# Router logits from the raw residual sums, and two weight pieces split ahead in borrowed places

## The chip, the cores and the metric

The program runs on one core of one Trainium2 chip. Its engines work side by side, each through its own instruction stream in order: TensorE (PE, with its weight loads PEld), VectorE (DVE), ScalarE (ACT), GpSimd (POOL) and SyncE (SP), which starts the weight transfers. The metric is the device time of one execution in microseconds (us), as a median over runs; lower is better.

## What is computed

Two layers over 256 rows of 1024 columns: layer 0 is a mixer and a dense SwiGLU; layer 1 is a gated DeltaNet mixer and a mixture of 8 SwiGLU experts, of which every row uses the best two. After each of the four sublayers comes `x <- LayerNorm(alpha * x + f(x))`. What the change touches is the end of the DeltaNet and the head of the experts:

```python
h = mixer_gated_deltanet(x, ...)                     # ends in  o @ w_out
x = layer_norm(ALPHA * x + h, c_ln1_g, c_ln1_b)      # (r - mean) * rstd * g + b
logits = x @ w_router + b_router                     # (256, 8)
top_val, top_idx = lax.top_k(logits, 2)
gates = softmax(top_val)
y = sum over e of combine[:, e] * swiglu(x, w_gu[e], w_down[e])
x = layer_norm(ALPHA * x + y, c_ln2_g, c_ln2_b)
```

With the raw sum `r = ALPHA * x + h`, its row mean and `rstd`, the logits are also `rstd * (r @ (g * w_router)) - mean * rstd * colsum(g * w_router) + colsum(b * w_router) + b_router`.

## The kernel before

The 256 rows are two blocks of 128 (block 0 and 1). Every float32 product runs as three matmuls: weights and activations are split into a rounded high part and the rest (`wh`, `wl`; `xh`, `xl`), ACT writing the high part and DVE (in a few places POOL) the low part. Weights come in pieces of 1 MB (`wraw`), started by SP in program order into raw places, 15 of them by the time of the experts; each piece is split in two halves of 1024 columns, which PE uses one after the other. The split halves live in a ring of five pairs of places, two of them in a pool that ends with the dense part, so three for the experts. The emitted order is made when the kernel is built: `presplit` splits ahead as far as the ring allows, and small pieces of work (the chunks of the DeltaNet, gathers, expert activations) are generators that `tick` puts between weight matmuls when a simple estimate of engine times (`Pace`) says that their inputs are ready. So a small piece that is added to the DeltaNet shifts where many later ones are put.

The DeltaNet starts with projections and a small chain (`sm`: decays and betas) and ends with `out_proj`: for each of the eight row groups k of the output weights PE multiplies block 0; block 1 follows at once for k below 4, and the last four k of block 1 come in `late`. `sublayer_end` then takes each block through `ln_block`: residual sum and statistics on DVE, square root on ACT, then the normalising steps shared by DVE, ACT and POOL. The normalised block is transposed by PE (`transposed`, four 128x128 transposes for each half) and copied to `xt` by ACT.

`route` takes it from there: eight router matmuls a block (`logits`, 8 columns each), the comparison of all pairs of logits on DVE (`chosen`: `e3`, `cnt`, `sel`), a count of the rows chosen ahead (`count` on PE), `slot` and the one-hot matrices `S` (`places`, `onehot` on DVE). Fills (`self.fill`, matmuls of the identity with itself whose result nobody reads) stand in between on PE. `natural_parts` makes the high and low parts `xnh` (ACT) and `xnl` (POOL) of the normalised block. PE then gathers the rows of experts 0 and 1 with `S` (`gather_block`, quarters 0 to 3, each with `xnh` and `xnl`), ACT and DVE copy them to `xgh` and `xgl`, and the first expert's gate and up matmuls begin as soon as two quarters are there (`G0 = 2`). One more half of weights is split ahead in the places `hh` and `hl` by `extra`, POOL writing its low part. `gates` computes the weights of the two experts: maximum and difference on DVE, exponential on ACT, then the switch of ACT to the table of the expert activation.

Of the kernel before, what the change touches and what calls it, by code (L numbers as in the profile page):

```python
# [16 lines left out]
T = 256  # L17
# [4 lines left out]
NE = 8  # L22
# [87 lines left out]
LQ = 4  # L110
HV = 512
SP0 = 640
SP3 = 1024
MG = -300.0
GT = 3
FI = 6, 3, 3
# [116 lines left out]
class Columns:  # L233

    def __init__(self, tiles):
        self.tiles = tiles

    def __getitem__(self, k):
        return self.tiles[k[2].start // 512]


class Net:
# [288 lines left out]
    def sublayer_end(self, pt, n, table, between=None, early=1, plain=False, split=None):  # L531
# [7 lines left out]
        if plain:  # L539
            xh, lo = lambda b, q: self.xpart(self.xt, b, q), lambda b, q: None  # L540
        else:
            lo = lambda b, q: nc.vector.tensor_sub(xl(b, q), tv[b, q], xh(b, q))
# [22 lines left out]
        if between:  # L565
            between(r, ready)
        else:
            for q in range(2):
                ready(1, q)
        self.x = r  # L570
# [43 lines left out]
    def out_proj(self, key, oh, ol, wait):  # L614
# [14 lines left out]
        for k in range(KT):  # L629
# [403 lines left out]
    def load_g1(self):  # L1033
# [12 lines left out]
        self.g1 = cwn, nea, dtb  # L1046

# [127 lines left out]
    def mixer1(self):  # L1175
# [44 lines left out]
        def prologue():  # L1220
# [3 lines left out]
            nc.vector.tensor_copy(cw, t[:, 0:96])  # L1224
            self.give()
# [383 lines left out]
        pt = self.out_proj("wo1", oh, ol, wait)  # L1609
        self.ring = [r for r in self.ring if r[0] is self.spl]  # L1610
        self.NSPL -= self.NDENSE
        self.xt = self.keep.tile([P, KT, T], F32, name="xt", tag="xh")
        self.e3 = self.keep.tile([P, 2048], F32, name="e3", tag="xl")[:, 0:2 * NE * NE].rearrange("p (b e f) -> p b e f", b=2, e=NE)
        self.sublayer_end(pt, 3, "natural_log_exp_and_others", self.route, plain=True, split=(SP0, SP3))
# [26 lines left out]
    def moe_open(self):  # L1641

        nc, a, tc = self.nc, self.a, self.tc
        self.raw_pool("raw2", RO)
        self.load_next()
        self.mo = mo = self.ctx.enter_context(tc.tile_pool(name="mo", bufs=1))
        self.wr = mo.tile([P, KT, NE], F32, name="wr")
        nc.gpsimd.dma_start(self.wr, a["moe_w_router"].rearrange("(k p) e -> p k e", p=P))
        self.br = mo.tile([P, NE], F32, name="br")
        nc.gpsimd.dma_start(self.br, a["moe_b_router"].partition_broadcast(P))  # L1650
# [17 lines left out]
    def route(self, r, ready):  # L1668
# [3 lines left out]
        tt, mm, X = nc.vector.tensor_tensor, nc.tensor.matmul, mybir.AxisListType.X  # L1672
        lg, e3, sel = self.lg, self.e3, self.sel
        p = self.ps("A")
        s = self.first = self.new_s()

        def logits(b, ks=range(KT)):
            for k in ks:
                mm(p[:, b * NE:(b + 1) * NE], self.xt[:, k, b * P:(b + 1) * P], self.wr[:, k], start=k == b == 0,
                   stop=k == KT - 1, skip_group_check=True)  # L1680

        def chosen(b):
            tt(lg[:, b], p[:, b * NE:(b + 1) * NE], self.br, OP.add)
            yield
            tt(e3[:, b], lg[:, b][:, None, :].to_broadcast([P, NE, NE]), lg[:, b][:, :, None].to_broadcast([P, NE, NE]),
               OP.subtract)
            yield
            tt(e3[:, b], e3[:, b], c("tie").rearrange("p (e f) -> p e f", e=NE), OP.is_gt)
            yield
            nc.vector.tensor_reduce(self.cnt[:, b], e3[:, b], axis=X, op=OP.add)  # L1690
            yield
            nc.vector.tensor_scalar(sel[:, b], self.cnt[:, b], 1.5, None, OP.is_lt)

        def count(b, m, start, stop):
            mm(p[:, (2 + b) * NE:(3 + b) * NE], m, sel[:, b if m is self.tri else 0], start=start, stop=stop,
               skip_group_check=True)

        def places(b):
            nc.vector.scalar_tensor_tensor(self.slot[:, b], p[:, (2 + b) * NE:(3 + b) * NE], 1.0, sel[:, b], OP.add, OP.mult)
            yield  # L1700
            for j in range(2):
                self.onehot(s, j, lambda b: self.slot[:, b, j:j + 1], (b,))
                yield

        fill = lambda n: self.fill(c("ident"), n)
        fill(FI[0])
        logits(0)
        self.natural_parts(0, r[0])
        ready(1, 0)
        fill(FI[1])  # L1710
        ready(1, 1)
        for _ in chosen(0):
            pass
        logits(1, range(0, LQ))
        count(0, self.tri, False, True)
        count(1, self.one, False, False)
        logits(1, range(LQ, KT))
        fill(FI[2])
        self.natural_parts(1, r[1])
        steps = [chosen(1), places(0)]  # L1720
        while steps:
            for g in list(steps):
                if next(g, 1):
                    steps.remove(g)
        self.early = [self.ps("B") for _ in range(4)]
        self.live += 4
        for i, t in enumerate(self.early):
            if i == 2:
                count(1, self.tri, False, True)
            self.gather_block(t, (self.xnh, self.xnl)[i % 2], s, i // 2, 0)  # L1730
        for _ in places(1):
            pass
        self.presplit(1)
        for b in range(2):
            nc.scalar.activation(r[b], r[b], AF.Copy, scale=ALPHA)
# [39 lines left out]
    def gather(self, s, xg, got, early=()):  # L1775

# [3 lines left out]
        early = list(early)  # L1780
        yield from self.when(s, slack=MG)
        for q in range(4):
            for i, xn in enumerate((self.xnh, self.xnl)):
                if early:
                    p = early.pop(0)
                else:
                    p = yield from self.take()
                    self.gather_block(p, xn, s, q, 0)
# [157 lines left out]
    def extra(self):  # L1946

        tiles = []
        for _ in range(2):
            for t in self.new_parts():  # L1950
                pass
            tiles.append(self.parts)
        self.ring.insert(0, (None, tiles))
        self.held = -1
        self.presplit(1, self.nc.gpsimd)

    def extra_done(self):
        self.hfree += 2

    def moe(self):  # L1960
# [15 lines left out]
        def prep(e):  # L1976
            xs = [self.new_xg() for _ in range(2)]
            xg[e], xg[e + 1] = xs
            yield from self.gather(S[e], xs, got[e], self.early if e == 0 else ())
# [9 lines left out]
        next(first)  # L1989
        self.extra()  # L1990
# [8 lines left out]
        self.y = self.x  # L1999

        def mult(e, c, u, after):
            pt = [self.ps("A") for _ in range(c[1] // 512)]
            n = 8 if c[1] == 1024 else 4
            for j in range(n):
                w = self.next(("gu", e, c, u))
                then = (lambda: after(pt)) if j == n - 1 else None
                if isinstance(w[0], Columns):
                    self.held, then = 0, self.extra_done
# [191 lines left out]
```

## Time and profile before

| | us |
|---|---|
| median of 3 runs | 1598.83 (1598.19 to 1599.57) |
| the profiled execution | 1597.8 |
| its span | 1596.0 |
| TensorE busy, sum of the page | 1555.4 |
| VectorE / ScalarE / GpSimd busy | 1301.3 / 1050.6 / 160.5 |

All rows are of the one profiled execution; times are counted from the start of its span. A timeline row gives the start, the duration, the engine, the operation with what it writes and reads, how many instructions it joins, and in brackets the idle time just before it with what ended that. On PE one logical float32 matmul is two instructions. A row of windows gives for one stretch its length, then busy time (and instructions) of PE, PEld, DVE, ACT and POOL, the granted TensorE clock as a share of 2.4 GHz, the busy share of the transfer engines, and GB/s.

### The profile page before, as it was taken

The numbers are of one execution on the slowest core, as the hardware profiler recorded it, in microseconds if no ns is written. First come the engines' busy times: TensorE is split into PE (matmuls) and PEld (weight loads), VectorE is DVE, ScalarE is ACT, GpSimd is POOL, SyncE is SP. The second block draws the span as 40 slices with busy tenths as digits, with TensorE's granted clock in tenths as the row PEclk, the third lists the DMA queues.
The fourth block names the chain that finished last, engine by engine and source line by source line (L and its number), as shares of the span: only waits on it lengthen the run. The fifth ranks groups of instructions, "written<-read, shape, count | busy, mean of one in ns | idle before, by whom it ended". The sixth has DMA issues, their size and how long they took to land.

```text
span 1596.0 us, 22720 instructions
## 1 busy us (share of the span) xinstructions
PE 1555.4 (97%) x8467; PEld 1332.8 (84%) x8467; DVE 1301.3 (82%) x1541; ACT 1050.6 (66%) x1239; POOL 160.5 (10%) x231
## 2 busy tenths in 40 slices
PE   9999999998999989999999999999999999999995
PEld 7788999997999968888888888888888888888884
DVE  5667555558867877999989999989999998999997
ACT  5345444445643347877877877878877778777774
POOL 5233000002361540000000000000000000000001
PEclk9999999999999989999999999999999999999998
DMA  7446555556313678999999999999999999999960
GB/s 265 134 159 223 190 198 192 185 168 198 97 47 106 226 275 294 376 370 350 372 347 341 367 368 362 367 362 335 369 368 363 360 375 328 369 366 368 361 219 28
DMA packets 161992, 444.81 MB, mean 279 GB/s; under 512 B 7553, under 2 KB 53778, under 8 KB 161874
## 3 DMA queue, kind: packets, MB, share of 16 engines
q1 hardware_dynamic: 160338, 437.98, 76.0%
q0 software_dynamic: 1536, 5.31, 1.1%
q8 instruction: 68, 1.11, 0.3%
q14 instruction: 50, 0.41, 0.1%
HBM read 442.21 MB, written 1.05 MB: 278 GB/s over the span
## 4 chain that ended last, share of the span: by engine, by line
PE 59%; issue 3%; DMA 0%; POOL 0%; DVE 0%; POOLq 0%; DVEq 0%
PE psA L223 37%; PE psB L223 21%; DMA gb<-in_c_ln_g_dram 0%; POOL x L223 0%; DVE wl L223 0%; POOLq L2196 0%; DVE xgl L223 0%; POOLq L223 0%; DVEq L223 0%
## 5 line engine op out<-in xcount | busy, mean ns | idle before, releaser
L223 DVE SCALAR_TENSOR_TENSOR wl<-wraw,wh 128x1024 fp32r<-128x1024 f32 (+2 forms) x824 | 992.7, 1223 | 199.0 <-ACT wh L223 147.1
L223 ACT ACTIVATE wh<-wraw 128x1024 fp32r<-128x1024 f32 (+3 forms) x835 | 863.1, 1052 | 265.2 <-PE psA L223 201.3
L223 PE MATMUL psA<-wh,xgh 128*128 128x512 f32 x894 | 291.0, 395 | 0.0
L223 PE MATMUL psA<-wh,xgl 128*128 128x512 f32 x894 | 288.3, 392 | 0.0
L223 PE MATMUL psA<-wl,xgh 128*128 128x512 f32 x894 | 279.4, 394 | 0.0
L223 PEld LDWEIGHTS psA<-wh,xgl 128*128 128x128 f32 x894 | 168.2, 188 | 37.2
L223 PEld LDWEIGHTS psA<-wh,xgh 128*128 128x128 f32 x894 | 166.9, 189 | 34.5
L223 PEld LDWEIGHTS psA<-wl,xgh 128*128 128x128 f32 x894 | 165.9, 188 | 34.8
L223 PE MATMUL psB<-wh,hh 128*128 128x512 f32 x560 | 183.3, 392 | 0.0
L223 PE MATMUL psB<-wh,hl 128*128 128x512 f32 x560 | 183.0, 392 | 0.0
L223 PE MATMUL psB<-wl,hh 128*128 128x512 f32 x560 | 182.8, 392 | 0.0
L223 PE MATMUL psA<-xh,wh 128*128 128x256 f32 x608 | 172.8, 284 | 0.0
L223 PE MATMUL psA<-xh,wl 128*128 128x256 f32 x608 | 170.0, 280 | 0.0
L223 PE MATMUL psA<-xl,wh 128*128 128x256 f32 x608 | 169.9, 280 | 0.0
L223 PEld LDWEIGHTS psB<-wh,hl 128*128 128x128 f32 x560 | 105.0, 188 | 23.5 <-DVE hl L223 0.9
L223 PEld LDWEIGHTS psB<-wl,hh 128*128 128x128 f32 x560 | 104.5, 188 | 22.3
L223 PEld LDWEIGHTS psB<-wh,hh 128*128 128x128 f32 x560 | 103.8, 188 | 20.6
L223 PEld LDWEIGHTS psA<-xh,wh 128*128 128x128 f32 x608 | 115.0, 189 | 1.4 <-issue 0.5
L223 PEld LDWEIGHTS psA<-xl,wh 128*128 128x128 f32 x608 | 115.0, 189 | 0.5
L223 PEld LDWEIGHTS psA<-xh,wl 128*128 128x128 f32 x608 | 115.0, 189 | 0.0
L223 POOL TENSOR_TENSOR x<-x,gb 128x256 f32<-128x256 f32 x4 | 4.2, 1069 | 993.8 <-ACT x L223 993.6
L223 PE MATMUL psA<-wh,xh 128*128 128x512 f32 (+4 forms) x224 | 74.1, 359 | 2.2 <-ACT wh L223 1.7
(298 smaller groups left out, 1449.5 us busy)
## 6 DMA issues: line engine op xcount, KB each, us to landing
wraw<-in_moe_w_gu_dram SPq DMA_DIRECT2D x224, 1024.0 KB, 6.2
wraw<-in_moe_w_down_dram SPq DMA_DIRECT2D x110, 1024.0 KB, 6.0
wraw<-in_ffn_w_gu_dram SPq DMA_DIRECT2D x26, 1024.0 KB, 5.1
wraw<-in_ffn_w_down_dram SPq DMA_DIRECT2D x14, 1024.0 KB, 4.9
wraw<-in_c_w_in_dram SPq DMA_DIRECT2D x12, 1024.0 KB, 5.7
wraw<-in_ab_w_in_dram SPq DMA_DIRECT2D x10, 1024.0 KB, 5.3
wraw<-in_ab_w_out_dram SPq DMA_DIRECT2D x4, 1024.0 KB, 4.9
wraw<-in_c_w_out_dram SPq DMA_DIRECT2D x4, 1024.0 KB, 7.0
```

The lines of the kernel that those rows point to most:

```text
L223: r = f(*args, **kw)
```

## The change

The router works on the raw sums. The router weights are loaded early (with the constants of the DeltaNet), multiplied by the gain, and the two column sums `wgt` are made in the prologue of the DeltaNet by four DVE operations, one matmul and two copies. `out_proj` hands its last work to `route`, which interleaves the late matmuls of block 1 with the transposes of the raw sums, so `xt` holds raw sums and the router matmuls need no LayerNorm. LayerNorm is done whole rows at a time on DVE beside them; POOL has no part in it, and `xnl` is made by DVE too. Both blocks are compared and counted together. Sixteen fills stand in one group ahead of the count. `gates` is begun, and its two table loads are issued, before the first copies of gathered rows. Three of the 15 raw places are lent: two hold the high and low parts of one weight half each (`wlent`), one holds `xt`; they go back as places for transfers later. The scaling of the residual by ALPHA moves behind the start of the experts, in four pieces.

```diff
@@ class Net, cut
-        if pool is None:
-            for q, (h, l) in enumerate(i_):
-                self.split(h[:, None], l[:, None], v[:, :, q * 512:(q + 1) * 512], eng)
-            return [Columns(x) for x in zip(*i_)]
+        if isinstance(i_, str):
+            w = pool.tile([P, 2048], F32R, name="wlent", tag=i_)
+            h, l = Lent(w[:, o:o + m].rearrange("p (a n) -> p a n", a=sa) for o in (0, 1024))
+            self.split(h, l, v, eng)
+            w = Lent((h, l))
+            w.place = pool, i_
+            return w
@@ out_proj
+        if end:
+            return end(pt, [lambda c, v=v: mm(1, c, *v) for v in late])
@@ load_g1
+        nc.gpsimd.dma_start(self.wr, a["moe_w_router"].rearrange("(k p) e -> p k e", p=P))
+        nc.gpsimd.dma_start(self.br, a["moe_b_router"].partition_broadcast(P))
+        for t, n in ((self.gp, "c_ln1_g"), (self.bp, "c_ln1_b")):
+            nc.gpsimd.dma_start(t, a[n].rearrange("(k p) -> p k", p=P))
@@ mixer1, prologue
+            for i, (w, v) in ((1, (wb, self.bp)), (0, (self.wr, self.gp))):
+                tt(w, self.wr, v[:, :, None].to_broadcast([P, KT, NE]), OP.mult)
+                nc.vector.tensor_reduce(self.wgs[:, i], w.rearrange("p k e -> p e k"), axis=mybir.AxisListType.X, op=OP.add)
+            yield from self.when(self.wgs)
+            t = yield from self.take()
+            mm(t[:, 0:16], c("one").to_broadcast([P, P]), self.wgs.rearrange("p a e -> p (a e)"), start=True, stop=True)
+            nc.vector.tensor_copy(self.wgt[:, 0], t[:, 0:8])
+            tt(self.wgt[:, 1], t[:, 8:16], self.br, OP.add)
+            self.give()
@@ moe_open
+        self.lent = [self.slots.pop() for _ in range(3)]
@@ route
-    def natural_parts(self, b, x):
-        self.nc.scalar.activation(self.xnh[b], x, AF.Copy)
-        self.nc.gpsimd.tensor_tensor(self.xnl[b], x, self.xnh[b].bitcast(F32), OP.subtract)
...
+        self.presplit(1)
+        self.ring = self.lent[:2] + self.ring
+        self.held -= 2
+        self.presplit(2)
+        self.table("sqrt_and_others")
...
+        for f in late:
+            f(0)
+        for i in range(2):
+            part(0, i)
+        for i in range(2):
+            self.ln_stats(r[0], st[0], i)
+        deviation(0)
+        for q in range(2):
+            turned(0, q)
+        part(1, 0)
+        self.ln_stats(r[1], st[1], 0)
+        centred(0)
+        scales(0)
+        for i, f in enumerate(late):
+            if i == 2:
+                turned(1, 0)
+            f(1)
+        normed(0)
...
+        part(1, 1)
+        logits(0, range(0, 4))
+        self.ln_stats(r[1], st[1], 1)
+        deviation(1)
+        turned(1, 1)
+        logits(0, range(4, 8))
+        logits(1, range(0, 4))
+        centred(1)
+        scales(1)
+        logits(1, range(4, 8))
+        normed(1)
+        for b in range(2):
+            stt(self.lt[:, b], self.wgt[:, 0], nb[b], self.wgt[:, 1], OP.mult, OP.add)
+        for b in range(2):
+            stt(lg[:, b], ps[b][:, 0:NE], rs[b], self.lt[:, b], OP.mult, OP.add)
...
+        for _ in range(FI):
+            mm(self.early[0][:, 0:P], c("ident"), c("ident"), start=True, stop=True)
+        count(0, self.tri, True, True)
+        count(1, self.tri, False, False)
+        count(1, self.one, False, True)
+        for i in range(2):
+            lows(0, i)
...
+        for i in range(2):
+            lows(1, i)
+        self.slots.append(place)
+        self.table("natural_log_exp_and_others")
+        self.weights = self.gates()
+        next(self.weights)
         self.presplit(1)
-        for b in range(2):
-            nc.scalar.activation(r[b], r[b], AF.Copy, scale=ALPHA)
+    def residuals(self):
+        for b in range(2):
+            for c in range(2):
+                x = self.x[b][:, c * 512:(c + 1) * 512]
+                self.nc.scalar.activation(x, x, AF.Copy, scale=ALPHA)
+                yield 4
@@ moe
-        self.extra()
...
-        gates = self.gates()
-        next(gates)
         self.spawn(first)
-        self.spawn(gates, 20)
+        self.spawn(self.weights, 20)
+        self.spawn(self.residuals(), 30)
```

Three places show what moves. On PE at the head of the experts (`cb` is the identity: `psB<-cb,x` are transposes, `psA<-cb` or `psB<-cb` fills; `wr,xt` are router matmuls, `sel` the counts, `S,xnh` and `S,xnl` gathers), before:

```order
L223 MATMUL psA<-wl,xh 128x512
L223 MATMUL psB<-cb,x_5882 128x128 x8
L223 MATMUL psA<-cb 128x128 x6
L223 MATMUL psA<-wr,xt 128x8 x8
L223 MATMUL psB<-cb,x_5883 128x128 x4
L223 MATMUL psA<-cb 128x128 x3
L223 MATMUL psB<-cb,x_5883 128x128 x4
L223 MATMUL psA<-wr,xt 128x8 x4
L223 MATMUL psA<-sel,c_5814 128x8
L223 MATMUL psA<-sel,cb 128x8
L223 MATMUL psA<-wr,xt 128x8 x4
```

The transposes follow the last weight matmul, and block 0 is counted between the two halves of block 1's router matmuls. The same place on PE after:

```order
L220 MATMUL psA<-wl,xh 128x512
L220 MATMUL psB<-cb,x_5875 128x128 x4
L220 MATMUL psA<-wh,xh 128x512
...
L220 MATMUL psA<-wr,xt 128x8 x4
L220 MATMUL psB<-cb,x_5875 128x128 x4
L220 MATMUL psA<-wr,xt 128x8 x12
L220 MATMUL psB<-cb 128x128 x16
L220 MATMUL psA<-sel,c_5824 128x8 x2
L220 MATMUL psA<-sel,cb 128x8
L220 MATMUL psB<-S,xnh 128x256 x4
```

Twelve of the sixteen transposes now stand among the late weight matmuls, all router matmuls are together, and one group of fills stands ahead of the three counts. On ACT, from the second copies of `xnh` to the first copies of gathered rows, before:

```order
L223 ACTIVATE xnh<-x_5883 128x1024
L223 ACTIVATE wh<-wraw 128x1024
L223 ACTIVATE x_5882<-x_5882 128x1024
L223 ACTIVATE x_5883<-x_5883 128x1024
L223 ACTIVATE hh<-wraw 128x512 x2
L223 ACTIVATE xgh<-psB 128x256 x4
L223 ACTIVATE comb<-comb 128x16
L223 ACT_TABLE_LOAD
```

Here the first four copies `xgh` come ahead of the exponential (`comb`) and its table load. The same place on ACT after:

```order
L220 ACTIVATE xnh<-x_5875 128x1024
L220 ACT_TABLE_LOAD
L220 ACTIVATE comb<-comb 128x16
L220 ACT_TABLE_LOAD
L220 ACTIVATE wh<-wraw 128x1024
L220 ACTIVATE xgh<-psB 128x256 x4
```

Two table loads, the exponential and one weight half now stand ahead of the first `xgh`. On DVE at the start of the DeltaNet, after (before, `sm<-psA,dtb` followed `cw<-psB` directly):

```order
L220 COPY cw<-psB 128x96
L220 TENSOR_TENSOR wb<-wr,bp 128x64
L220 TENSOR_REDUCE wgs<-wb 128x8
L220 TENSOR_TENSOR wr<-wr,gp 128x64
L220 TENSOR_REDUCE wgs<-wr 128x8
L220 TENSOR_TENSOR sm<-psA,dtb 128x8
```

Four operations now stand ahead of the small chain `sm`.

## Rows read from the trace of the kernel before

**Rows 1.** The page's first line, the span.

```profile
span 1596.0 us, 22720 instructions
```

**Rows 2.** Who waited for whom between 597 us and the end, in total: on PE, and on SP's queue (waiting engine, what it was to do, the engine waited for; us in total, times, longest).

```profile
PE psB L223 <- DVE xgl L223: 0.6, 1, 0.6
...
SPq L223 <- DVE wl L223: 790.1, 319, 8.8
```

**Rows 3.** Windows: one stretch of 50 us in the middle of the experts.

```profile
1000.00:1050.00 50.00, 50.00 (x225) 41.12 (x224) 46.18 (x46) 40.04 (x42) 0.00 (x0) 1.00 1.01 374
```

**Rows 4.** Timeline of PE from the late matmuls of the output projection to the experts.

```profile
571.18 0.39 PE L223 MATMUL psA<-wh,xh 128*128 128x512 f32 x1
...
576.52 0.40 PE L223 MATMUL psA<-wl,xh 128*128 128x512 f32 x1
...
578.17 1.50 PE L223 MATMUL psA<-cb 128*128 128x128 f32 x12
579.51 1.85 PE L223 MATMUL psA<-wr,xt 128*128 128x8 f32 x16
581.52 0.65 PE L223 MATMUL psB<-cb,x 128*128 128x128 f32 x4 [0.16 <-DVE x L223]
582.01 0.83 PE L223 MATMUL psA<-cb 128*128 128x128 f32 x6
...
587.75 0.59 PE L223 MATMUL psA<-sel,c 128*128 128x8 f32 x2 [3.33 <-DVE sel L223]
...
588.62 1.85 PE L223 MATMUL psA<-wr,xt 128*128 128x8 f32 x8
...
595.11 0.47 PE L223 MATMUL psB<-S,xnh 128*128 128x256 f32 x2 [1.10 <-DVE S L223]
...
597.66 1.05 PE L223 MATMUL psA<-wh,xgh 128*128 128x512 f32 x2
...
604.14 0.63 PE L223 MATMUL psA<-hh,xgh 128*128 128x512 f32 x2
```

**Rows 5.** Timeline of DVE over the same stretch.

```profile
570.70 0.69 DVE L223 SCALAR_TENSOR_TENSOR x<-x,psA 128x512 f32<-128x512 f32 x1 [3.27 <-PE psA L223]
...
572.74 0.69 DVE L223 BATCH_NORM_STATS2 st<-x 128x6 f32<-128x512 f32 x1
...
573.71 0.75 DVE L223 SCALAR_TENSOR_TENSOR x<-x,mv,bc 128x512 f32<-128x512 f32 x1
...
583.02 2.18 DVE L223 TENSOR_TENSOR e<-lg 128x64 f32<-128x64 f32 x1
585.24 0.23 DVE L223 TENSOR_TENSOR e<-e,c 128x64 f32<-128x64 f32 x1
...
585.75 1.94 DVE L223 TENSOR_SCALAR sel<-cnt 128x8 f32<-128x8 f32 x1
...
591.63 0.17 DVE L223 TENSOR_SCALAR sel<-cnt 128x8 f32<-128x8 f32 x1
...
593.28 1.69 DVE L223 TENSOR_SCALAR S<-c,slot 128x128 fp32r<-128x128 f32 x2
594.89 1.21 DVE L223 SCALAR_TENSOR_TENSOR wl<-wraw,wh 128x1024 fp32r<-128x1024 f32 x1
596.02 1.40 DVE L223 CAST xgl<-psB 128x256 fp32r<-128x256 f32 x4
```

**Rows 6.** Timeline of POOL over the same stretch.

```profile
582.46 2.67 POOL L223 TENSOR_TENSOR xnl<-x,xnh 128x1024 fp32r<-128x1024 f32 x1 [2.40 <-ACT xnh L223]
585.28 2.39 POOL L223 TENSOR_TENSOR xnl<-x,xnh 128x1024 fp32r<-128x1024 f32 x1 [0.15 <-ACT xnh L223]
```

**Rows 7.** Timeline of ACT around the start of the experts.

```profile
597.75 0.21 ACT L223 ACTIVATE comb<-comb 128x16 f32<-128x16 f32 x1 [0.91 <-DVE comb L223]
597.97 1.28 ACT L223 ACT_TABLE_LOAD   x1
599.26 0.66 ACT L223 ACTIVATE xgh<-psB 128x256 fp32r<-128x256 f32 x2
...
601.01 1.06 ACT L223 ACTIVATE wh<-wraw 128x1024 fp32r<-128x1024 f32 x1
```

**Rows 8.** Windows of 1 us at the head of the experts; the granted clock is the third number from the end.

```profile
588.00:589.00 1.00, 1.00 (x6) 1.00 (x7) 0.00 (x0) 0.76 (x1) 0.00 (x0) 0.50 0.00 0
...
594.00:595.00 1.00, 0.01 (x1) 0.00 (x0) 1.00 (x2) 0.00 (x0) 0.88 (x1) 1.00 1.03 426
...
597.00:598.00 1.00, 1.00 (x5) 1.00 (x6) 0.68 (x4) 0.25 (x2) 0.00 (x0) 0.60 1.04 422
...
600.00:601.00 1.00, 1.00 (x5) 0.87 (x5) 0.00 (x0) 0.54 (x2) 0.00 (x0) 0.69 1.04 422
601.00:602.00 1.00, 1.00 (x7) 0.83 (x6) 0.00 (x0) 1.00 (x2) 0.00 (x0) 1.00 0.20 70
```

**Rows 9.** Timelines at the start of the DeltaNet: the copy on DVE that ends the chain `sm` there, then the matmuls on PE that wait behind it.

```profile
393.52 0.17 DVE L223 COPY sm<-psB 128x16 f32<-128x16 f32 x1
...
394.19 1.16 PE L223 MATMUL psB<-c,sm 128*128 128x128 f32 x8 [2.08 <-ACT sm L223]
```

**Rows 10.** One of PE's waits between 400 and 597 us (as in rows 2), then a window over the main stretch of the DeltaNet.

```profile
PE psB L223 <- POOL ED L223: 0.7, 1, 0.7
...
400.00:500.00 100.00, 98.82 (x836) 97.23 (x836) 75.72 (x123) 51.97 (x96) 45.40 (x37) 1.00 0.27 82
```

More of the change, by code (lines that the diff above doesn't have):

```diff
@@ L529, in residual, with sublayer_end @@
         self.nc.vector.scalar_tensor_tensor(t[:, cs], x[:, cs], ALPHA, pt[c], OP.mult, OP.add)
-    def sublayer_end(self, pt, n, table, between=None, early=1, plain=False, split=None):
+    def sublayer_end(self, pt, n, table, between, early=1, split=None):
         nc = self.nc
@@ L564, in sublayer_end @@
         self.ln_block([lambda: res(1, 0), second], r[1], lambda: lo(0, 1), split and split[1], table)
[L565 to L569, printed above, removed]
+        between(r, ready)
         self.x = r
@@ L612, in plan_out, with out_proj @@
             self.plan(key, w[2 * q * P:(2 * q + 2) * P].rearrange("(a p) n -> p a n", p=P))
-    def out_proj(self, key, oh, ol, wait):
+    def out_proj(self, key, oh, ol, wait, end=None):
         pt = [[self.ps("A") for _ in range(2)] for _ in range(2)]
@@ L1607, in wait @@
                 self.moe_open()
[L1609 to L1614, printed above, removed]
+        self.out_proj("wo1", oh, ol, wait, self.route)
     def gate_up(self, w, c, u):
@@ L1661, in moe_open, with route, part, deviation @@
         self.cnt = mo.tile([P, 2, NE], F32, name="cnt")
-    def natural_parts(self, b, x):
-        self.nc.scalar.activation(self.xnh[b], x, AF.Copy)
-        self.nc.gpsimd.tensor_tensor(self.xnl[b], x, self.xnh[b].bitcast(F32), OP.subtract)
-    def route(self, r, ready):
+    def route(self, pt, late):
         nc, c = self.nc, self.c
-        tt, mm, X = nc.vector.tensor_tensor, nc.tensor.matmul, mybir.AxisListType.X
-        lg, e3, sel = self.lg, self.e3, self.sel
+        tt, stt, mm, X = nc.vector.tensor_tensor, nc.vector.scalar_tensor_tensor, nc.tensor.matmul, mybir.AxisListType.X
+        lg, sel = self.lg, self.sel
+        self.presplit(1)
[3 more added lines that the diff above has]
+        self.table("sqrt_and_others")
+        r = [self.new_x(3, b) for b in range(2)]
+        place = self.lent[2]
+        xt = place[0].tile([P, 2048], F32, name="xt", tag=place[1]).rearrange("p (b k n) -> p b k n", b=2, k=KT)
+        st = [self.ln.tile([P, 2, 6], F32, name="st") for _ in range(2)]
+        mv = [self.ln.tile([P, 2], F32, name="mv") for _ in range(2)]
+        rs = [self.ln.tile([P, 1], F32, name="rs") for _ in range(2)]
+        nb = [self.ln.tile([P, 1], F32, name="nb") for _ in range(2)]
+        g, bv = self.gb
+        def part(b, i):
+            self.residual(r[b], self.x[b], pt[b], i)
+        def deviation(b):
+            nc.vector.bn_aggr(mv[b], st[b].rearrange("p a b -> p (a b)"))
+            nc.scalar.activation(rs[b], mv[b][:, 1:2], AF.Sqrt, bias=c("eps"))
+        def scales(b):
+            nc.vector.reciprocal(rs[b], rs[b])
+            stt(nb[b], mv[b][:, 0:1], -1.0, rs[b], OP.mult, OP.mult)
+        def turned(b, q):
+            t = self.ps("B")
+            self.transpose4(t, r[b][:, q * 512:(q + 1) * 512])
+            nc.scalar.activation(xt[:, b, 4 * q:4 * q + 4], t.rearrange("p (a n) -> p a n", a=4), AF.Copy)
+        def centred(b):
+            stt(r[b], r[b], mv[b][:, 0:1], g, OP.subtract, OP.mult)
+        def normed(b):
+            stt(r[b], r[b], rs[b], bv, OP.mult, OP.add)
+            nc.scalar.activation(self.xnh[b], r[b], AF.Copy)
+        def lows(b, i):
+            cs = slice(i * 512, (i + 1) * 512)
+            tt(self.xnl[b][:, cs], r[b][:, cs], self.xnh[b][:, cs].bitcast(F32), OP.subtract)
+        for f in late:
[16 more added lines that the diff above has]
+        normed(0)
+        self.held -= len(late)
+        self.ring = [v for v in self.ring if v[0] is self.spl]
+        self.NSPL -= self.NDENSE
+        ps = [self.ps("A") for _ in range(2)]
@@ L1674, in route @@
         p = self.ps("A")
-        s = self.first = self.new_s()
+        e3 = self.keep.tile([P, 2048], F32, name="e3", tag="xl")[:, 0:2 * NE * NE].rearrange("p (b e f) -> p b e f", b=2, e=NE)
         def logits(b, ks=range(KT)):
             for k in ks:
[L1679 to L1692, printed above, removed]
@@ L1694, in count @@
-        def count(b, m, start, stop):
[L1695 to L1700, printed above, removed]
+                mm(ps[b][:, 0:NE], xt[:, b, k], self.wr[:, k], start=k == 0, stop=k == KT - 1, skip_group_check=True)
+        def count(b, m, start, stop):
+            mm(p[:, b * NE:(b + 1) * NE], m, sel[:, b if m is self.tri else 0], start=start, stop=stop, skip_group_check=True)
@@ new lines, in route @@
+        ef = lambda t: t.rearrange("p b e f -> p b (e f)")
+        tt(e3, lg[:, :, None, :].to_broadcast([P, 2, NE, NE]), lg[:, :, :, None].to_broadcast([P, 2, NE, NE]), OP.subtract)
+        tt(ef(e3), ef(e3), c("tie")[:, None, :].to_broadcast([P, 2, NE * NE]), OP.is_gt)
+        nc.vector.tensor_reduce(self.cnt, e3, axis=X, op=OP.add)
+        nc.vector.tensor_scalar(sel, self.cnt, 1.5, None, OP.is_lt)
+        self.early = [self.ps("B")]
+        for _ in range(FI):
+            mm(self.early[0][:, 0:P], c("ident"), c("ident"), start=True, stop=True)
@@ L1701, in places @@
+        count(0, self.tri, True, True)
[3 more added lines that the diff above has]
+            lows(0, i)
+        s = self.first = self.new_s()
+        stt(self.slot, p[:, 0:2 * NE].rearrange("p (b e) -> p b e", b=2), 1.0, sel, OP.add, OP.mult)
+        for b in range(2):
             for j in range(2):
                 self.onehot(s, j, lambda b: self.slot[:, b, j:j + 1], (b,))
-                yield
-        fill = lambda n: self.fill(c("ident"), n)
@@ L1706, in route @@
[L1706 to L1732, printed above, removed]
+        for i in range(2):
[4 more added lines that the diff above has]
+        next(self.weights)
@@ L1783, in gather @@
             for i, xn in enumerate((self.xnh, self.xnl)):
[L1784 to L1788, printed above, removed]
+                p = yield from self.take()
+                self.gather_block(p, xn, s, q, 0)
                 self.gather_block(p, xn, s, q, 1)
@@ L1944, in scatter, with lent_back @@
             self.hfree += len(parts) == 2
[L1946 to L1958, printed above, removed]
+    def lent_back(self, place):
+        self.slots.append(place)
+        self.load_next()
     def moe(self):
@@ L1978, in prep @@
             xg[e], xg[e + 1] = xs
-            yield from self.gather(S[e], xs, got[e], self.early if e == 0 else ())
+            yield from self.gather(S[e], xs, got[e])
         def run(gen):
@@ L2006, in mult @@
                 then = (lambda: after(pt)) if j == n - 1 else None
-                if isinstance(w[0], Columns):
-                    self.held, then = 0, self.extra_done
+                if isinstance(w, Lent):
+                    self.held += 1
+                    then = lambda w=w: self.lent_back(w.place)
                 self.gate_up_mm(pt, c, xg[e], j, w, then, got[e & ~1])
```

35 lines of the change are left out of this document (14 added, 21 removed).

## The prediction

> **What bounds the kernel now.** I read the waits first, then the windows, then the timelines of one place. From 597 us on PE waits for nothing but one 0.6 us copy, while SP spends 790 us waiting for DVE to free raw places [rows 2]; a window in the middle of the experts has PE busy for all 50 us at the full clock while the transfers run at 374 GB/s [rows 3]. So the experts, some 985 us, are bound by PE, the transfers follow it, and a gain at their head is kept to the end. In the DeltaNet PE is busy for 98.8 of 100 us [rows 10]. The 1596.0 us span [rows 1] has its loose stretch between the last late matmul, which starts at 576.52, and the first expert matmul at 597.66 [rows 4]. There PE follows DVE: it waits 3.3 us for `sel` of block 0 and 1.1 us for `S` of block 1 [rows 4].
>
> Three things make this stretch long. LayerNorm stands ahead of the transposes and so of the logits. DVE is held up while POOL works: the comparison of 64 columns took 2.18 us where the next operation of that shape took 0.23, and `sel` 1.94 where its twin took 0.17 [rows 5]; the long ones end with the two `xnl` on POOL, at 585.13 and 587.67 [rows 6]. Last, PE idles and then runs at 0.50 of its clock, the lower of its two levels (1.2 GHz): the granted clock was 0.50 in the stretch from 588, full again at 594, 0.60 in the stretch from 597, after PE had been nearly idle from 594, 0.69 from 600 and full from 601 [rows 8]; so the second spell lasted from about 597.2 to 600.6. At that level eight instructions of the router took the 1.85 us in which sixteen had been done [rows 4].
>
> **The change, part by part: when the choice of experts is known.** I carry the old times on, since `out_proj` up to 571.2 is the same. Late matmuls go at 0.232 us (24 from 571.18 to 576.75) and four transposes at 0.49 (581.52 to 582.01) [rows 4]. PE: 12 late ones to 574.0, eight transposes to 575.0, six late ones to 576.4, four transposes to 576.9, six late ones to 578.2. DVE: residuals of block 0 from 570.7 and statistics (0.69 each [rows 5]) to 573.7; the first half of block 1 waits for PE until 574.1 and ends at 575.5; the two normalising steps of block 0 are 1024 wide, at 1.25 each (between the 1.21 of a split and twice 0.75 [rows 5]), with the small ones to 578.3. Its last residual waits for PE's 578.2; then statistics to 580.0, centring, scales and normalising to 582.9, four 8-column operations of about 0.15 to 583.5, four comparisons of 128 columns at about 0.3 to 584.7. The old `sel` of block 1 ended at 591.8 [rows 5], so the choice comes 7.1 us earlier. The added splits of two weight halves (1.06 on ACT, 1.21 on DVE [rows 5, 7]) lie before 570.7, where DVE waited 3.3 us [rows 5]: nothing, and up to 0.5 if their piece is late. With POOL silent I take no stalls on DVE; one would cost up to 2.
>
> **What holds it back.** PE reaches the sixteen fills after one more group of transposes and twelve router matmuls of two instructions (0.23 each [rows 4]), at 582.5. Six fills took 1.34 us (578.17 to 579.51), so sixteen take 3.6 and the counts 0.7: `slot` can begin at 586.8, 2.1 after `sel` where 0.8 would do. `S` is there from 587.5, PE has gathered two quarters by about 590.3, and then it waits. Behind `S` on DVE stand the low parts of block 1 (1.2) and the maximum and difference for `gates` (0.4), to 589.8. ACT has nothing to copy until the exponential, which waits for these: 0.21, table load 1.28, weight half 1.06, first `xgh` 0.33 [rows 7], to 592.7. DVE splits the low part of that half (1.21) before its first `xgl` (0.35 [rows 5]). With hand-overs the first full product can go on at 594.1. Before, the first expert matmul stood at 597.66 [rows 4], so of 7.1 us about half is left.
>
> From 594.1 at the full clock, 18 expert matmuls and 16 gathers of half the width take 6.0, to 600.1. At that point all gathers are done, 16 high and 4 low products. Before, all gathers were done at 604.14 with four high products fewer [rows 4]; with 0.9 for these, 605.0. **Difference: 4.9 us.**
>
> On the table load the trace and a page can be set side by side. The exponential ends at 597.96, the load starts at 597.97 and the next copy starts at 599.26, so a switch costs 1.28 [rows 7]. The Trainium skill's "ScalarE: Activation LUTs", "What ACT_TABLE_LOAD costs", adds a drain of some 1.38 us for every switch. By that page the load in this chain would cost 2.66, and by an estimate from it the gain would be 3.5 in place of 4.9; no such drain stands between the rows, and I keep 4.9.
>
> **The clock.** PE will again be idle for 2.7 us (590.3 to 593.0 or so) and short of work around it, after 8 us without a gap thanks to the fills. Before, nearly idle stretches of this length were followed by the lower level twice [rows 8], so I expect one spell. The one from 597.2 to 600.6 halved work for 3.4 us and cost 1.7. In the new one part is idle anyway: 1.3, between 0 (it falls wholly into the wait) and 3.4 (two spells in dense work).
>
> **The DeltaNet.** Four small DVE operations (0.23 each [rows 5]) and two copies stand ahead in the chain that PE waits 2.08 us for [rows 9]: its end comes 1.3 later, PE has six more matmuls to do before it, 0.7, so 0.6 is lost, between 0 and 1.3. The rest is order: chunks of the solves move by several weight matmuls. PE's idle time there is 1.2 us in 100 [rows 10]; I take 0, between -1.2 and +2. Early loads of the router weights on POOL's queue have 230 us to land, far from any reader: 0. The scaling of the residual moves from 586 into ACT's idle time among the experts: 0. The lent places leave three fewer for transfers around 590, where the window from 588 shows none moving [rows 8], since no place was free: 0, and about 1 if a piece comes late.
>
> **The sum.** -4.9 + 1.3 + 0.6 = -3.0 on the profiled execution's 1597.8: 1594.8. That execution lies 1.0 under the median of 1598.83. Where spells of the lower clock fall may differ from run to run, so I add half of that: **1595.3**.
>
> **Rivals.** *Clock kept:* the spell misses the dense work and nothing is lost. Sum -4.3, or -5.5 with idle time saved in the DeltaNet: 1592.8 to 1594.0. For it speaks the dense group of fills; against it the 2.7 us wait behind ACT. *Two spells:* PE goes at 1.2 GHz through gathers and first products; -4.9 + 3.4 + 0.6 = -0.9: 1597.4, no change. Before had two spells with a like pattern. *ACT or a weight half later than I have it* (a drain, a late piece): +1.4, about 1596.7. *Slower, by order:* the solves of the DeltaNet now come in smaller groups, with one weight group between a product and the next that needs its copy. A hand-over that isn't covered costs some 0.7, as the one wait for `ED` does [rows 10]. Four such eat the gain, ten make it 7 us: -3.0 + 7.0 = +4.0, 1602.3. It decides when successive groups belong to the same unit; against it, four units are in flight and PE was nearly always covered with them before.
>
> **How the numbers follow.** Forecast 0.45, clock kept 0.20, two spells 0.18, ACT or a half late 0.07, order 0.10. A measurement here can tell about 0.2% from no change: under 1595.6 is faster, over 1602.0 slower. The forecast lies on that line, and I give 0.28 of it to faster. So faster 0.48, same 0.42, slower 0.10. The range takes in kept clock and two spells with their margins and leaves out the order rival and the best end: 1592.4 to 1599.0.
>
> **What would show it.** Right: `sel` 6 to 8 us earlier after the late matmuls, no DVE operation of 8 to 128 columns over 0.5 us, PE idle between the second quarter of gathers and the first `xgh` with ACT in exponential, table load and `wh`, one spell at 0.50. Wrong: PE waits in the DeltaNet totalling more than 3 us over the old ones, PE waiting for a transfer after 597, a first expert matmul as late as 597, or none of ACT's chain in the way.

## The result, and the profile after

| | us | ratio to before |
|---|---|---|
| before, median of 4 runs | 1599.14 (1598.19 to 1599.57) | |
| changed kernel, median of 4 runs | 1618.25 (1616.81 to 1622.68) | 1.0125 [1.0105, 1.0145] |
| its profiled execution | 1616.81, span 1615.0 | |

It is 19 us slower; 1595.3 was forecast, with 1592.4 to 1599.0 as the range. The page's first lines of the changed kernel show the longer span with PE busier than before (1575.8 against 1555.4 us), not waiting more:

```profile
span 1615.0 us, 22739 instructions
...
PE 1575.8 (98%) x8477; PEld 1334.8 (83%) x8477; DVE 1300.1 (80%) x1547; ACT 1050.3 (65%) x1239; POOL 153.3 (9%) x226
```

PE's waits from 597 us to the end, all of them (as in [rows 2]):

```profile
PE psA L220 <- ACT xgh L220: 2.3, 1, 2.3
PE psA L220 <- DVE xgl L220: 0.6, 1, 0.6
```

So the loss has to be in time in which PE works. Laid beside each other from mark to mark (first and last matmul of layer 0's FFN, PE's 0.9 us wait for `xl` in the output projection, end), the two profiled executions differ so: up to the FFN 0.2, FFN 223.3 and 228.1, DeltaNet 201.4 and 203.4, from the output projection to the end 1030.3 and 1042.3. Nearly all of it lies in stretches that the change doesn't touch. Two windows in which PE is busy throughout, one of the FFN and one of the experts, first of the kernel before, then of the changed one (columns as in [rows 3]):

```profile
150.00:345.00 195.00, 195.00 (x1397) 183.26 (x1396) 102.66 (x95) 86.00 (x94) 0.00 (x0) 1.00 0.57 190
700.00:1500.00 800.00, 799.81 (x3632) 657.85 (x3632) 737.64 (x699) 633.91 (x702) 0.00 (x0) 1.00 0.97 360
```

```profile
150.00:345.00 195.00, 195.00 (x1366) 182.58 (x1365) 101.28 (x94) 84.72 (x92) 0.00 (x0) 1.00 0.57 190
700.00:1500.00 800.00, 799.91 (x3573) 646.44 (x3572) 727.86 (x689) 624.69 (x691) 0.00 (x0) 1.00 0.97 354
```

At the same full clock PE gets through 1366 matmuls where it did 1397, and 3573 where it did 3632. Busy share says nothing here; the count of instructions does. The timelines of PE in the FFN, before and then after, show it one by one. The pitch, the time from one matmul's start to the next one's, is 0.113 us, then 0.120.

```profile
199.88 0.28 PE L223 MATMUL psA<-xl,wh 128*128 128x256 f32 x1
199.99 0.28 PE L223 MATMUL psA<-xh,wl 128*128 128x256 f32 x1
200.10 0.28 PE L223 MATMUL psA<-xh,wh 128*128 128x256 f32 x1
200.22 0.28 PE L223 MATMUL psA<-xl,wh 128*128 128x256 f32 x1
```

```profile
199.85 0.28 PE L220 MATMUL psA<-xl,wh 128*128 128x256 f32 x1
199.97 0.28 PE L220 MATMUL psA<-xh,wl 128*128 128x256 f32 x1
200.09 0.29 PE L220 MATMUL psA<-xh,wh 128*128 128x256 f32 x1
200.21 0.28 PE L220 MATMUL psA<-xl,wh 128*128 128x256 f32 x1
```

1.65% (3632 over 3573) of some 975 us of experts is 16.1 us, 2.3% of the FFN's 223 is 5.1; the routing stage gives about 4 back.

In this profile the routing stage itself went as forecast. PE of the changed kernel, from the first late matmul (the place of 571.18 in [rows 4]):

```profile
578.15 0.40 PE L220 MATMUL psA<-wh,xh 128*128 128x512 f32 x1
...
589.07 3.82 PE L220 MATMUL psB<-cb 128*128 128x128 f32 x32
...
594.34 0.87 PE L220 MATMUL psB<-S,xnh 128*128 128x256 f32 x4 [0.88 <-DVE S L220]
...
599.02 0.73 PE L220 MATMUL psA<-wh,xgh 128*128 128x512 f32 x2 [2.33 <-ACT xgh L220]
600.34 0.73 PE L220 MATMUL psA<-wh,xgl 128*128 128x512 f32 x2 [0.59 <-DVE xgl L220]
...
608.06 0.62 PE L220 MATMUL psA<-wlent,xgh 128*128 128x512 f32 x2
```

Its DVE (as [rows 5]) and its ACT (as [rows 7]):

```profile
591.37 0.17 DVE L220 TENSOR_SCALAR sel<-cnt 128x16 f32<-128x16 f32 x1
...
593.50 0.17 DVE L220 SCALAR_TENSOR_TENSOR slot<-psA,sel 128x16 f32<-128x16 f32 x1 [0.76 <-PE psA L220]
```

```profile
596.11 0.22 ACT L220 ACTIVATE comb<-comb 128x16 f32<-128x16 f32 x1 [3.96 <-DVE comb L220]
596.34 1.28 ACT L220 ACT_TABLE_LOAD   x1
597.64 1.06 ACT L220 ACTIVATE wh<-wraw 128x1024 fp32r<-128x1024 f32 x1
598.60 1.19 ACT L220 ACTIVATE xgh<-psB 128x256 fp32r<-128x256 f32 x4
```

And windows of 1 us for the clock (as [rows 8]): full while PE idles at 597, 0.61 from 601, 0.69 from 604, one spell.

```profile
597.00:598.00 1.00, 0.00 (x0) 0.00 (x0) 0.00 (x0) 0.99 (x2) 0.00 (x0) 1.00 0.00 0
...
601.00:602.00 1.00, 1.00 (x7) 0.90 (x6) 1.00 (x2) 0.27 (x1) 0.00 (x0) 0.61 0.87 78
604.00:605.00 1.00, 1.00 (x5) 0.84 (x4) 0.00 (x0) 0.66 (x2) 0.00 (x0) 0.69 1.07 430
```

### The profile page after: what moved, and what is told of

Its sections match the earlier page's. It is cut to its first block, busy times and chain, and to the rows that moved or that the text cites. A ratio compares the mean times of both kernels' runs of the same rounds, so it can differ in the third digit from the quotient of the medians.

```text
span 1615.0 us, 22739 instructions
## 1 busy us (share of the span) xinstructions
PE 1575.8 (98%) x8477; PEld 1334.8 (83%) x8477; DVE 1300.1 (80%) x1547; ACT 1050.3 (65%) x1239; POOL 153.3 (9%) x226
## 4 chain that ended last, share of the span: by engine, by line
PE 67%; issue 4%; POOL 2%; DVE 2%; ACT 1%; DMA 0%; POOLq 0%; DVEq 0%; ACTq 0%
PE psA L220 41%; PE psB L220 25%; POOL nt L220 1%; DVE wl L220 1%; DMA gb<-in_c_ln_g_dram 0%; ACT et L220 0%; POOL V L220 0%; POOL Pm L220 0%; POOL x L220 0%; POOL grs L220 0%; ACT wh L220 0%; POOL gate L220 0%; DVE y L220 0%; DVE ED L220 0%; DVE gate L220 0%
## 5 line engine op out<-in xcount | busy, mean ns | idle before, releaser
L220 PEld LDWEIGHTS psA<-xh,wh 128*128 128x128 f32 x608 | 115.3, 190 | 1.5 <-issue 0.7
```

The lines of the kernel that those rows point to most:

```text
L220: r = f(*args, **kw)
```

## The experiments

The change puts six new tiles into the pool `const`, the first on its side of SBUF (the on-chip memory): `wr` with 256 bytes a partition, `br`, `gp` and `bp` with 32 each, `wgs` and `wgt` with 64 each, 480 in all. Every tile behind them moves up by 480: in the compiled kernels the first `wh` of the pool `spl` (the places of split weights) lies at byte 41632 before and 42112 after. **Theory A** is that this alone makes PE slower; **theory B** that the new instructions, their order, the early transfers or the lent places do.

**1. The kernel before, moved.** `e1`, `e3` and `e4` only widen the first constant tile, by 120, 8 and 16 columns:

```diff
 def load_const(self, n, pool, eng):
-    t = pool.tile([P, CONST[n].shape[1]], F32, name=n)
-    eng.dma_start(t, self.a[n])
+    m = CONST[n].shape[1]
+    t = pool.tile([P, m + (120 if n == "cb" else 0)], F32, name=n)
+    eng.dma_start(t[:, 0:m], self.a[n])
```

> The kernel before, with nothing but 480 unused bytes per partition behind the first constants, so that every later tile of that side (raw places, the split weight places in spl, xe, ln, raw2) begins 480 bytes higher, as it does in the changed kernel; instructions and their order stay the same. Theory A (addresses: a matmul's pitch depends on where its operands begin, and the new constants moved the weight places): slower by 17 to 22 us, about 1618, with 128x256 matmuls that read the places in spl starting every 120 ns instead of 113 to 118 and the 512-wide pairs of the experts every 467 ns instead of 457. Theory B (the new instructions, their order, the early transfers or the lent places slow PE): 1599, within 0.2%, pitches as before. Theory C (half and half): 1605 to 1612.

Measured: 1620.23, ratio 1.0142 [1.0127, 1.0156]. The windows of `e1`:

```profile
150.00:345.00 195.00, 195.00 (x1363) 182.44 (x1363) 100.80 (x93) 84.38 (x92) 0.00 (x0) 1.00 0.55 184
700.00:1500.00 800.00, 799.81 (x3576) 646.19 (x3575) 727.42 (x688) 624.24 (x691) 0.00 (x0) 1.00 0.95 354
```

Not one instruction of the change is in it, and its counts are within three of the changed kernel's. Theory A is enough for the whole loss; what theory B adds is left to `e2`.

> The kernel before with 32 unused bytes per partition: the weight places begin at a multiple of 64 bytes, as in the changed kernel, instead of 32 past one. Theory A1 (what counts is the place within 64 bytes): as slow as the shift by 480, 1616 to 1620. Theory A2 (what counts is a longer pattern, 128 or 256 bytes): a time of its own, anywhere from 1590 to 1620. Theory B: 1599.

> The kernel before with 64 unused bytes per partition: the place within 64 bytes is that of the kernel before, within 128 it is the other half. Theory A1 (64 bytes): 1599, pitches as before. Theory A2 (128 bytes or more): a time of its own, anywhere from 1590 to 1620. Theory B: 1599.

Measured: `e3` 1617.08, 1.0120 [1.0105, 1.0134]; `e4` 1615.82, 1.0107 [1.0092, 1.0122]. A shift by 64 is slow as well, so it isn't the place within 64 bytes.

**2. The changed kernel, moved back.** `e2` has the same edit with 8 columns (32 bytes), on the changed kernel.

> The changed kernel with 32 more unused bytes per partition behind the first constants, so that the later tiles lie 512 bytes higher than in the kernel before instead of 480, and every address of a weight place is the same as before modulo 512. Theory A (addresses, with a pattern that repeats within 512 bytes): pitches as in the kernel before, and the time is that of the prediction's sum, 1594 to 1598. Theory B (instructions or order): 1617 to 1620, as the changed kernel. If the pattern is longer than 512 bytes, something between, with pitches that differ from both.

Measured: 1596.52 (1591.62 to 1600.01), ratio 0.9992 [0.9980, 1.0004]. The windows again:

```profile
150.00:345.00 195.00, 195.00 (x1396) 183.26 (x1396) 103.48 (x95) 86.14 (x95) 0.00 (x0) 1.00 0.58 193
700.00:1500.00 800.00, 799.87 (x3634) 658.09 (x3633) 738.12 (x699) 634.52 (x702) 0.00 (x0) 1.00 0.96 360
```

32 more bytes take 22 us off the changed kernel: without the shift, its instructions and order cost nothing that these runs can tell. What is left of the change is worth 1.3 us, between 3.2 less and 0.6 more; the forecast of 3.0 less lies in that.

**3. Which tiles.** `e5` puts the 480 bytes behind `spl`:

```diff
     self.spl = pool(name="spl", bufs=1)
+    pad = pool(name="pad", bufs=1).tile([P, 120], F32, name="pad")
+    tc.nc.gpsimd.memset(pad, 0.0)
     self.xe = pool(name="xe", bufs=2)
```

> The kernel before with the same 480 unused bytes, but put behind the split weight places (spl) instead of ahead of them: the raw places and the weight places stay where they were, all that follows on that side (xe, ln, the raw places raw2, the DeltaNet's inverse tiles, xnh and xnl) begins 480 bytes higher. One short write to the unused bytes is added on POOL at the start. If it is the address of the weight places that counts: 1598, within 0.2%, pitches of the FFN and experts as in the kernel before. If it is any of the tiles behind them (the raw places that DVE and ACT read while PE works, or the transfers that write them): 1612 to 1620, as with the shift of all.

Measured: 1597.92, 0.9998 [0.9988, 1.0008].

```profile
150.00:345.00 195.00, 195.00 (x1396) 183.27 (x1395) 102.93 (x95) 86.20 (x94) 0.00 (x0) 1.00 0.56 189
700.00:1500.00 800.00, 799.78 (x3633) 657.84 (x3632) 737.92 (x700) 634.47 (x703) 0.00 (x0) 1.00 0.96 360
```

The counts are those of before: moving what lies behind the weight places by 480 does nothing.

**4. Place or distance.** Modulo 256 bytes the gathered operands `xgh`, `xgl`, `hh`, `hl` of the experts begin at 96 in both kernels, `wh` and `wl` of `spl` at 160 before and at 128 in the changed one. `e9` leaves the weight places there and moves the gathered operands, in the pool `mb`, by 224 bytes, to 128 as well:

```diff
-    sc = self.mb.tile([P, 2, 2], F32, name="sc")
+    sc = self.mb.tile([P, 60], F32, name="sc")[:, 0:4].rearrange("p (a b) -> p a b", a=2)
```

> The changed kernel with its weight places where the change put them, and 224 unused bytes per partition at the top of the pool mb instead, so that the gathered operands (xgh, xgl, hh, hl), which are loaded as weights in the experts, begin at the same place modulo 256 as wh and wl (128 and 128). Theory R (the pitch depends on the distance between the two operands' beginnings modulo 256; distances 0 and 64 gave 228 to 229 ns for 512 columns, all others that occur 233): the experts' pitch falls from 233.3 to 228 or 229 and the time by 14 to 19 us, to 1599 to 1604, while the FFN keeps its slow 120 ns. Theory S (what counts is where the weight places begin, by itself): 1618, pitches as in the changed kernel.

Measured: 1595.97, 0.9987 [0.9977, 0.9996].

```profile
150.00:345.00 195.00, 195.00 (x1374) 182.94 (x1373) 99.87 (x92) 84.53 (x93) 0.00 (x0) 1.00 0.57 191
700.00:1500.00 800.00, 799.88 (x3664) 663.20 (x3663) 742.43 (x705) 639.73 (x708) 0.00 (x0) 1.00 0.96 363
```

The FFN stays slow (1374), the experts are faster than in any kernel so far (3664): theory R. The time lies 3 us under the 1599 to 1604 that theory R was to give, since the pitch at distance 0 came out lower than the 228 to 229 put in. What counts is the distance between where the streamed operand of a matmul and the operand loaded as weights begin. All eight distances in steps of 32 bytes modulo 256 occur in these traces. Mean pitch of 512-column matmuls at the full clock (the under 2% of starts that were over 260 ns apart are left out):

| begin of streamed less begin of loaded, mod 256 | ns | where |
|---|---|---|
| 0 | 227.2 | experts of `e9` (and of `e11`, below) |
| 64 | 229.2 | experts of before and `e2` |
| 32, 96, 128 | 233.3, 233.3, 232.7 | experts of the changed kernel, `e3`, `e4` |
| 160, 192, 224 | 233.9, 233.2, 233.5 | projections of the changed kernel; projections of before; down products of the changed kernel's FFN |

The same distance at other places gives nearly the same pitch. Over all runs here, distance 0 took 227 to 229 with both operands at 128, 160, 192 or 224 modulo 256; 64 took 229 with the loaded one at 96 or 160; 32 took 233 with it at 96, 160 or 192. So it is the distance, and not where either operand begins.

**5. The change's own terms, at the old addresses (base `e2`).** `e6`, then `e7`, then `e8`:

```diff
 def prologue():
...
-    yield from self.when(self.wgs)
-    t = yield from self.take()
-    mm(t[:, 0:16], c("one").to_broadcast([P, P]), ...)
-    nc.vector.tensor_copy(self.wgt[:, 0], t[:, 0:8])
-    tt(self.wgt[:, 1], t[:, 8:16], self.br, OP.add)
-    self.give()
...
 def route(self, pt, late):
...
+    t = self.ps("B")
+    mm(t[:, 0:16], self.one, ...)
+    nc.vector.tensor_copy(self.wgt[:, 0], t[:, 0:8])
+    tt(self.wgt[:, 1], t[:, 8:16], self.br, OP.add)
     for f in late:
         f(0)
```

```diff
-FI = 16
+FI = 2
```

```diff
     for i in range(2):
         lows(0, i)
+    self.presplit(1)
     s = self.first = self.new_s()
...
     self.weights = self.gates()
-    next(self.weights)
-    self.presplit(1)
     self.x = r
...
     self.spawn(first)
+    next(self.weights)
     self.spawn(self.weights, 20)
```

> The changed kernel at the old addresses (32 more bytes, run e2_after_512) with one step moved: the small product for the LayerNorm terms and its two copies stand at the head of the routing stage instead of at the start of the DeltaNet. If PE's new wait of 2.4 us for wgs there is a loss: PE gets from the end of the FFN to the last wait of out_proj about 2 us sooner than in e2, 201.7 instead of 203.7, and the time is 1594.0 to 1595.0. If that wait only stands in for the 2.1 us wait for sm of the kernel before, which comes back: at most 0.5 less than e2, 1596.0 to 1596.5.

Measured: 1597.38, 0.9999 [0.9987, 1.0010]. PE's waits in the DeltaNet, of `e2` and then of `e6`:

```profile
PE psB L220 <- DVE wgs L220: 2.4, 1, 2.4
```

```profile
PE psB L220 <- ACT sm L220: 2.1, 1, 2.1
...
PE psB L220 <- issue: 1.0, 1, 1.0
```

The wait for `wgs` only stood in for that for `sm`; without it the old one is back. The time, 0.9 over that of `e2` where up to 0.5 less was expected, doesn't differ from it by these intervals.

> The changed kernel at the old addresses with 2 fill matmuls instead of 16 ahead of the counts. If the fills hold the counts up, slot begins 0.8 to 1.0 us after sel instead of 2.1 (full clock) or 5.2 (half clock, e2's profile), and with it the gathers and the exponential's chain on ACT: 1.3 to 4 less, 1592.5 to 1595.5. If their use, to keep PE's clock up through the gathers and the first products, outweighs that: spells at 0.50 lie over the gathers in most executions and the time is that of e2 or above, 1596.5 to 1599.

> The changed kernel at the old addresses with ACT's order altered at the head of the experts: the next weight half and its low part ahead of slot, and the copies xgh of the first two quarters ahead of the exponential and the table load behind it. If ACT's chain (exponential, table load 1.28, wh 1.06) is what PE waits for between the second quarter of gathers and the first product, the wait of 2.3 us goes to under 0.7, and the time falls by 1.5 to 2.5 against e2: 1594.0 to 1595.0. If something else comes last there (the copies of the low parts behind wl on DVE, or the transfer of the next pieces): less than 0.7, 1596 or above.

Measured: `e7` 1594.68, 0.9977 [0.9968, 0.9987]; `e8` 1594.05, 0.9972 [0.9963, 0.9981]. The fills' price depends on the clock: 3.82 us at the full one (above), 6.70 in `e2`'s profile, at 0.50 of it:

```profile
584.72 6.70 PE L220 MATMUL psB<-cb 128*128 128x128 f32 x32
```

```profile
584.00:588.00 4.00, 4.00 (x20) 4.00 (x20) 3.86 (x11) 2.34 (x2) 0.00 (x0) 0.50 0.48 147
```

In `e7` the clock is at 0.50 for longer, from 584 to 596, over the counts, the first gathers and the first products:

```profile
584.00:588.00 4.00, 2.96 (x13) 2.57 (x12) 3.48 (x13) 2.34 (x2) 0.00 (x0) 0.50 0.56 190
588.00:592.00 4.00, 3.44 (x16) 3.47 (x16) 2.27 (x8) 1.64 (x3) 0.00 (x0) 0.50 0.18 72
592.00:596.00 4.00, 2.97 (x8) 1.76 (x8) 3.05 (x6) 2.96 (x6) 0.00 (x0) 0.50 0.18 23
```

Even so its median is 1.8 under that of `e2`. The two intervals overlap, so it is not shown to be faster; that the fills gain anything is not shown either. `e8` is 2.5 under `e2`, and their intervals just touch. In `e8` the wait of 2.3 for `xgh` is gone; its first product stands right behind the gathers:

```profile
595.23 0.64 PE L220 MATMUL psB<-S,xnh 128*128 128x256 f32 x4
595.71 0.63 PE L220 MATMUL psA<-wh,xgh 128*128 128x512 f32 x2
```

**6. A version that beats both.** `e10` is `e7` and `e8` together, `e11` adds 192 bytes in `mb` (the edit of `e9` with 52 columns in place of 60: distance 0). `e12` adds to that, in the pool `keep` (and lets two small tiles share one, to make room):

```diff
-    return self.keep.tile([P, D], F32, name="bc", tag="bc", bufs=2)
+    return self.keep.tile([P, D + 8], F32, name="bc", tag="bc", bufs=2)[:, 0:D]
...
-    self.xl = self.keep.tile([P, KT, T], F32R, name="xl")
+    self.xl = self.keep.tile([P, KT * T + 48], F32R, name="xl")[:, 0:KT * T].rearrange("p (k t) -> p k t", k=KT)
```

> The changed kernel at the old addresses with both edits of e7 and e8: 2 fills instead of 16, and the copies ahead of the exponential. If the fills and ACT's chain are two waits in a row, the gains add (1.8 and 2.5 under e2's 1596.5): 1592.0 to 1592.8. If they hide behind one another, the better of the two: 1594.

> e10 with 192 unused bytes at the top of mb, so that the distance between wh or wl and the gathered operands is 0 modulo 256 instead of 64; nothing else changes. Theory R with the pitches read so far (228.4 at distance 0, 229.2 at 64, 512 columns, some 4000 such matmuls in the experts): 2.5 to 4 less than e10, about 1589. If 0 and 64 are alike: as e10. Theory S: as e10.

> e11 with the two weight places in the pool keep put at a distance of 64 from xh and xl as well (they were at 0), by 64 and 192 unused bytes in that pool; mx shares a small tile with t1 to make room. Matmuls of 256 columns that load these places took 119.7 ns where those that load the places in spl, at a distance of 64, took 115.3; there are some 720. Theory R: these go to 115.3, 3.2 less, against up to 1.2 more in the projections of 512 columns where the distance becomes 192: 1.5 to 3 less than e11, about 1587. Theory S: as e11.

Measured: `e10` 1592.66, 0.9965 [0.9951, 0.9978]; `e11` **1583.97**, 0.9914 [0.9900, 0.9928]; `e12` 1586.24, 0.9926 [0.9911, 0.9940]. `e10` fits the sum of the two gains (1.8 + 2.5 off 1596.5), and none of its executions is as slow as the 1594 of the other case; each of the two steps by itself is near the noise. The distance took 8.7 us more off, clear of it, over twice what I expected, since at 0 the pitch is 227.2 and not the 228.4 that I had read from short stretches of other stages:

```profile
700.00:1500.00 800.00, 799.88 (x3664) 663.17 (x3663) 741.67 (x704) 638.82 (x707) 0.00 (x0) 1.00 0.96 363
```

`e12` missed: 1.5 to 3 less was forecast, and it came out 2.3 over `e11` (their intervals overlap). With all weight places at a distance of 64, the 256-column matmuls took 117.6 to 117.8 ns on average, between the 115.3 and the 119.7 that the two kinds had taken, and the 512-column projections rose from 228.5 to 233.2. For 256 columns the distance alone is not the rule (in the kernel before, groups at 64 ran at either 113 or 118 ns); what else is, stays open.

## Why the prediction was wrong, point by point

**The step that failed** is "Early loads of the router weights on POOL's queue have 230 us to land, far from any reader: 0." I priced the transfers and not the place that they take. The tiles put 480 bytes ahead of the weight places, the distance to the gathered operands went from 64 to 32 modulo 256 and the experts' pitch from 229.2 to 233.3 ns. `e1` shows that this is enough to make the old kernel slow, `e2` that undoing it is enough to make the changed one fast, `e9` that moving the other operand does it too. No rival had it: all of them argued with waits, order and clock, and this 0 was given no bounds.

The Trainium skill, "TensorE: Matmul & The Clock Gate", section "Step-by-step: what each phase is for", says that TensorE has two independent read ports, so that loading the next weights takes no read bandwidth from the running matmul. In the traces the two operands are not independent: with nothing changed for the experts but where the loaded operand begins (changed kernel and `e9`), the pitch is 233.3 or 227.2 ns. Whether read bandwidth or something else lies behind it, no run here shows.

**When the choice is known.** Right: `sel` ends 13.4 us after the first late matmul (578.15 to 591.54), forecast 13.5 (571.18 to 584.7), before 20.6 [rows 4, 5]. No small DVE operation took over 0.5.

**What holds it back.** Right: `slot` began 15.35 after that matmul (forecast 15.6), PE idled 2.33 for `xgh` behind exponential, table load and weight half, and the first full product stood at 22.2 (forecast 22.9). `e8` shows that this chain was the wait. All gathers and 20 products were done at 29.9; before it was 33.8 by the prediction's count: 3.9 won, against 3.6 forecast with the spell. The fills' term is too small for executions in which they run at the lower clock: they were priced at the full one, and in `e2`'s profile took nearly twice that.

**The table load.** 1.28, and the next operation 0.02 behind it (596.34, 597.64): again nothing stands between. The 1.38 of drain that the Trainium skill, "ScalarE: Activation LUTs", "What ACT_TABLE_LOAD costs", adds is not in these rows.

**The clock.** One spell, as forecast, in the changed kernel's profile; two in `e2`'s (one of them on the fills). From the output projection to the end `e2`'s profiled execution is only 1.8 us shorter than that of before (1028.5 against 1030.3). Executions of `e2` run from 1591.62 (mean granted clock 0.995) to 1600.01 (0.989), so much hangs on the spells.

**The DeltaNet.** Forecast 0.6 more, measured 2.0 in the changed kernel's profile and 2.3 in `e2`'s, inside the bounds of the two terms together but above the value: the chain's term was too small or the order's, put at 0, was. In `e2`'s profile that 2.3 takes back the 1.8 won behind it. `e2`'s has a spell at the lower clock (386 to 389) near the start there; `e12`'s, without one but with other distances, is 1.0 over before. `e1`, with the old order at the new places, took 2.0 more there too, but with a spell of its own (398 to 402). So how the changed kernel's 2.0 divides between the slower matmuls and order isn't separated.

**The order rival** (ten uncovered hand-overs) named the right sign and the wrong place: PE's waits in the DeltaNet grew by less than 1 us.

## What to carry to other kernels

Before pricing a new constant or a resized tile at nothing, look at which tiles lie behind it: here 480 bytes cost 19 us, and 32 more gave them back. When a PE-bound kernel changes its time everywhere at once, count matmuls per window at equal clock before looking for waits. For streams of 512-column matmuls of float32r (the type of the high and low parts), put both operands at the same place modulo 256 bytes: here worth 8.7 us of 1592.7.

## What was not expected of the hardware

The pitch of back-to-back 128x512 matmuls, each with weights of its own, depends on the distance between the beginnings of the two operands in a partition: 227.2 ns at 0 in the experts (228 to 229 in shorter streams), 229.2 at 64, 232.7 to 233.9 at the other six steps of 32 bytes modulo 256. For 256 columns groups of matmuls took 113 to 122 ns in patterns that the distance doesn't explain alone. VectorE and ScalarE operations were not touched by the shift: `wl` took 1.22 us and `wh` 1.06 in both kernels.
